# Stores, weights and a norm around the end of a recurrent head group: four moves in a hybrid diffusion step

## The chip, the cores and the metric

The kernel runs on one core of a Trainium2 chip. The metric is the time of one execution in microseconds (us), the median of several runs. Engine names: PE is TensorE (matrix products; PEld is its weight load), DVE is VectorE, ACT is ScalarE, POOL is GpSimd, SP is SyncE. Here SP, ACT and, after the change, POOL also issue DMA transfers, each in the order of its own queue.

## What is computed

One layer of a flow-matching backbone for 128 context tokens and 1024 latent tokens, all in float32. In the reference, cut to what matters here:

```python
h = rmsnorm(x, norm1_w) * (1 + sc1) + sh1
aq, ak, av, mq, mk, mv, mo, mg = split(h @ w_in)
attn_o = attention(q, keys, vals)                      # 8 heads of 64, softmax
hm = mlstm_bidir(q, k, v, gates, ...)                  # 4 heads of 128, two directions, chunks of 128
hm = rmsnorm(hm, mlstm_norm_w) * sigmoid(mo)
x = x + g1 * (concat([attn_o, hm]) @ w_out)
h2 = rmsnorm(x, norm2_w) * (1 + sc2) + sh2
x = x + g2 * (silu(gate) * up) @ w_down                # gate, up = h2 @ w_gu
y = rmsnorm(x, final_norm_w)
```

sh, sc and g come from a product of SiLU(cond) with `w_ada`; context and latent tokens have different ones. The final states of the context scan and the context's keys and values are outputs too.

## The kernel before

The 1152 tokens are nine blocks of 128: block 0 is the context, blocks 1 to 8 are latent. Three blocks make a chunk (chunks 0, 1, 2). Products are kept near float32 by splitting each operand into a high and a low part, so that one product is three matrix products (high x high, high x low, low x high). Splitting a weight takes a cast on ScalarE (`whi`, or `ir` for the early output weights) and a subtraction on VectorE (`wlo`, or `ir`); `load_piece` issues the load on SyncE's queue and then both.

The stages around the change, in order of the program:

1. `head_project(h)` makes q, k, v and the output gate of mLSTM head h for all blocks, and updates the chunk states block by block. It runs interleaved with the scan of head h - 1 and with attention of chunk 0. For every block it copies the transposed k (`kT`) out of PSUM on ScalarE.
2. `head_mlstm(h)` is the scan over the nine blocks. For a block it makes the decay weights (`dt` on ScalarE, `sd` on VectorE), the state part (`it` on ScalarE), the sum `nu`, the divisor `dn`, and the row `hm`, which GpSimd multiplies by the gate and, for finished blocks, by the norm factor (L897). The last head (`alone`) ends a chunk at a time and stores each chunk to the scratch tensor `hm_d[c]`: chunk 0 by SyncE's queue, chunks 1 and 2 by ScalarE's. The earlier heads store all chunks at the end by SyncE's queue.
3. Beside the last scan, `attn_out_first` multiplies chunk 0's attention output with the upper half of `w_out`, adds the gated result to x, and stores the residual rows to the scratch tensors `x1a_d[i]`. Its four weight pieces (two for each half n of the output columns) come by `load_piece`. The stores are collected in the list `stores` and issued on ScalarE's queue after the scan has been emitted. The `ada` generator streams more of `w_ada` at the same time.
4. `prefill` goes over blocks 0 to 8. `mix(b)` loads the block's row of `hm_d` (`hmr`, two ahead), transposes it on PE and splits it (`mx`). `half(b, n)` multiplies it with the lower half of `w_out` and adds the gated result. `end(b)` takes, for blocks 0 to 2, the mean square (`stats`), and emits the second norm (`norm2`) of chunk 0's block b - 1. `norm2` scales the row (`y`), transposes it on PE, applies scale and shift (`fl`) and splits it (`aTh`, `aTl`). Attention of chunk 1 is interleaved.
5. The feed-forward over the chunks follows, with `w_gu` and `w_down` streamed.

The program is written as generators that are interleaved by `weave`; the order on each engine is then set at build time by a scheduler that follows a simulated timeline and prefers older instructions, or those raised by `hot(n)`. Tiles of one tag are handed out in the order of the program; in these stages PSUM has three or four banks of the tag `mm`. Each engine works strictly in its order, so an instruction whose data are late holds all behind it, and a DMA issue that waits holds its queue's engine. `tc.issue_after(ins)` puts what is written inside it behind `ins` in the order of the engine of `ins`, without a wait for it.

Of the kernel before, what the change touches and what calls it, by code (L numbers as in the profile page):

```python
# [8 lines left out]
F32 = mybir.dt.float32  # L9
# [10 lines left out]
P = 128  # L20
# [8 lines left out]
NH = 4  # L29
# [4 lines left out]
CB = 3  # L34
NCH = NB // CB
CT = CB * P
# [9 lines left out]
def hybrid_step(ctx: ExitStack, tc: tile.TileContext, I: dict, O: dict):  # L46
    nc = tc.nc
    mm = nc.tensor.matmul
    act = nc.scalar.activation
    dve = nc.vector  # L50
    pool = nc.gpsimd
    dma = nc.sync.dma_start
# [46 lines left out]
    drp = ctx.enter_context(tc.tile_pool(name="drp", bufs=1, space=DRAM, reuse_waits="tile"))  # L99
# [4 lines left out]
        return psum["mm"].tile([P, 512], F32, name=nm("mm"), tag="mm")  # L104

    q_d = [drp.tile([P, 512], F32, name=f"q_d{b}") for b in range(NB)]
    hm_d = [drp.tile([CT, 512], F32, name=f"hm_d{c}") for c in range(NCH)]
    g_d = drp.tile([2, 2, D], F32, name="g_d")
    x1a_d = [drp.tile([P, D], F32, name=f"x1a_d{i}") for i in range(CB)]
    x1_d = [drp.tile([P, D], F32, name=f"x1_d{i}") for i in range(CB)]  # L110
# [633 lines left out]
    def head_project(h, st):  # L744

        w = groups_in[h + 1]
        pieces = w.made or w.pairs()
        w.inverses()
        nxt_steps = groups_in[h + 2].ready() if h + 1 < NH else iter(())
        next(nxt_steps, None)  # L750
        st["q"] = [None] * NCH
        st["b"] = [None] * NB

        def evac(b, ps):
            kt = mlp.tile([P, P], F32, name=nm("kt"), tag="kt", bufs=2)
            act(kt, ps[:, 0:P], AF.Copy, scale=w.inv_k)
            va = mlp.tile([P, P + 1], F32, name=nm("va"), tag="va", bufs=MB)
            act(va[:, 0:P], ps[:, P : 2 * P], AF.Copy, scale=w.inv)
            pool.memset(va[:, P : P + 1], 1.0)
            th = mlp.tile([P, P], F32, name=nm("th"), tag="th", bufs=1)  # L760
            act(th, ps[:, 2 * P : 3 * P], AF.Tanh, scale=w.inv_half)
            so = mlp.tile([P, P], F32, name=nm("so"), tag="so", bufs=MB)
            pool.tensor_tensor(out=so, in0=th, in1=mwh[:, h * P : (h + 1) * P], op=ALU.mult)
            pool.tensor_tensor(out=so, in0=so, in1=mwh[:, h * P : (h + 1) * P], op=ALU.add)
            pt = bank()
            transpose(pt[:, 0:P], kt)
            kT = mlp.tile([P, P], F32, name=nm("kT"), tag="kT", bufs=MB)
            nc.scalar.copy(kT, pt[:, 0:P])
            st["b"][b] = (kT, va, so)
            update(b, kt, va)  # L770

        st["s"] = states = {}
        st["raw"] = raws = {}
        for d in range(2):
            c0 = mlp.tile([P, P + 1], F32, name=nm("c0"), tag=("c0f", "c0b")[d], bufs=2 - d)
            dma(c0[:, 0:P], I["state_C"][0, 0, d, h])
            dma(c0[:, P : P + 1], I["state_n"][0, 0, d, h].rearrange("(p o) -> p o", o=1))
            states[d, 1 if d == 0 else NBL] = c0

        def update(b, kt, va):  # L780

            wv = mlp.tile([P, 2, P + 1], F32, name=nm("wv"), tag="wv", bufs=2)
            for d in range(2):
                pool.tensor_tensor(out=wv[:, d], in0=va, in1=qcol(1, d, b, h).to_broadcast([P, P + 1]), op=ALU.mult)
            pc = bank()
            mm(pc[:, 0 : 2 * (P + 1)], kt, wv.rearrange("p d x -> p (d x)"), start=True, stop=True)
            for d in range(2):
                if b == (NBL if d == 0 else 1):
                    continue
                add = pc[:, d * (P + 1) : (d + 1) * (P + 1)]  # L790
                cn = mlp.tile([P, P + 1], F32, name=nm("cs"), tag="cs", bufs=CSB)
                if d == 0 and b > 0:
                    dve.scalar_tensor_tensor(out=cn, in0=states[0, b], scalar=decb[:, b * 4 + h : b * 4 + h + 1], in1=add,
                                             op0=ALU.mult, op1=ALU.add)
                    states[0, b + 1] = cn
                    continue
                nc.scalar.copy(cn, add)
                if b > 0:
                    raws[b] = cn
                    continue  # L800
                dma(O["new_state_C"][0, 0, d, h], cn[:, 0:P])
                dma(O["new_state_n"][0, 0, d, h].rearrange("(p o) -> p o", o=1), cn[:, P : P + 1])

        def q_group(cs):
            banks = [bankA() for _ in cs]
            for k in range(KD):
                wh, wl = pieces[k // 2]
                for ps, c in zip(banks, cs):
                    mm(ps[:, 0:CT], wh[:, k % 2, 0:P], hTh[c][:, k, :], start=(k == 0), stop=False)
                    mm(ps[:, 0:CT], wh[:, k % 2, 0:P], hTl[c][:, k, :], start=False, stop=False)  # L810
                    mm(ps[:, 0:CT], wl[:, k % 2, 0:P], hTh[c][:, k, :], start=False, stop=(k == KD - 1))
                yield
            for ps, c in zip(banks, cs):
                qT = mlp.tile([P, CT], F32, name=nm("qT"), tag="qTm", bufs=2 * NCH)
                dve.tensor_scalar(out=qT, in0=ps[:, 0:CT], scalar1=w.inv, scalar2=None, op0=ALU.mult)
                st["q"][c] = qT

        for c in range(NCH):
            yield from q_group((c,))
        for i, _ in enumerate(linear_tok(pieces, P, 3 * P, evac, SINGLES)):  # L820
            if i % 6 == 5:
                next(nxt_steps, None)
            yield
        emit(nxt_steps)

    def head_mlstm(h, st):
# [30 lines left out]
        for b in range(NB):  # L857
# [34 lines left out]
            if b in ends:  # L892
                b0 = ends[b]
                n = b + 1 - b0
                v = hm[:, b0 : b + 1, :]
                r = rsqrt(mlp, ssh[:, b0 : b + 1], n, 1.0 / P)
                pool.tensor_tensor(out=v, in0=v, in1=bc(r, 2, [P, n, P]), op=ALU.mult)  # L897
                for c in range(b0 // CB, b // CB + 1):
                    (nc.scalar.dma_start if h == NH - 1 and c > 0 else dma)(hm_d[c][:, h * P : (h + 1) * P].rearrange("(b p) n -> p b n", p=P), hm[:, c * CB : (c + 1) * CB, :])
            yield  # L900


# [247 lines left out]
    def prefill(cur, nxt):  # L1150
# [4 lines left out]
        def load_hm(b):  # L1155
            if b >= NB:
                return None
            hm = xp.tile([P, 512], F32, name=nm("hmr"), tag="hmr", bufs=2)
            dma(hm, hm_d[b // CB][b % CB * P : (b % CB + 1) * P, :])
            return hm  # L1160

        def load_x1(b):
# [41 lines left out]
        def end(b):  # L1204
            if b < CB:
                with hot(200):
                    cur["rs"] += stats(x1s[0][b : b + 1])
            if 0 < b <= CB:
                yield from norm2(0, cur, b - 1)

        for b in range(2):
            mix(b)
# [15 lines left out]
                yield  # L1228
            yield from end(b)

    def attn_out_first(oT, ready, stores):


        x1 = hTp.tile([P, CB, D], F32, name="x1a", tag="hT2")
# [15 lines left out]
        def out():  # L1250
            for n in range(2):
                cs = slice(n * 512, (n + 1) * 512)
                ws = []
                for j in range(2):
                    rows = w_out[2 * j * P : (2 * j + 2) * P, cs].rearrange("(a p) n -> p a n", p=P)
                    ws.append(load_piece([(full_view, rows)], (2, 512), raw=raws[j], own=(his[j], los[j])))
                for cnd in range(2):
                    dma(gt[:, 2 * n + cnd], g_d[0, cnd : cnd + 1, cs].to_broadcast([P, 512]))
                yield
                for i in range(CB):  # L1260
                    while i not in ready:
                        yield
                    th, tl = mx[:, i, 0:4], mx[:, i, 4:8]
                    if n == 0:
                        dma(x1[:, i], xrow(i))
                        nc.scalar.copy(th, oT[i])
                        sub(tl, oT[i], th.bitcast(F32), "pool")
                        yield
                    ps = out_block([ws], 0, th, tl)
                    v = x1[:, i, cs]  # L1270
                    dve.tensor_tensor(out=gt[:, 4], in0=ps, in1=gt[:, 2 * n + (i > 0)], op=ALU.mult)
                    pool.tensor_tensor(out=v, in0=v, in1=gt[:, 4], op=ALU.add)
                    yield
                    if n == 1:
                        stores.append((x1a_d[i], x1[:, i]))

        return out(), ada

# [166 lines left out]
    oT = []  # L1445
# [5 lines left out]
        weave(head_project(h, sts[h]), beside((scan, 0.42), (att, 0.11)), 96, 96)  # L1451
        emit(scan)
    scan = head_mlstm(NH - 1, sts[NH - 1])
    stores = []
    first, ada = attn_out_first(oT, done, stores)
    emit(att)
    oT = []
    att = attention(1, oT, set())
# [1 line left out]
    emit(first)  # L1460
    emit(ada)
    emit(scan)
    for out, v in stores:
        nc.scalar.dma_start(out, v)
    es1.close()
    es_wp.close()
    es_d.close()
# [121 lines left out]
```

## Time and profile before

| | |
|---|---|
| median of 3 runs | 1564.69 us (1562.04 to 1565.68) |
| profiled execution | 1563.28 us, span of its instructions 1561.5 us |
| mean clock granted to TensorE | 0.98 |
| busy: PE, PEld, DVE, ACT, POOL | 1484.1, 1251.8, 1017.1, 772.3, 264.9 us |
| DMA queue of SyncE | 384670 packets, 230.26 MB |
| DMA queue of ScalarE | 3096 packets, 5.16 MB |

The profile is one execution. Busy time counts instructions of an engine; waits are put down to the event that came last. A row of the timeline has the start, the length, the engine, the line of the program, the operation, what it writes and reads, and, in brackets, how long the engine had been idle and what ended it. ACTq, SPq and POOLq are DMA issues or waits on those engines. The last head's scan ends near 506 us of the span; `prefill` lies between about 496 and 600 us, the feed-forward behind it.

### The profile page before, as it was taken

How to read it: one execution, taken by the hardware profiler on the slowest of the kernel's cores; microseconds unless marked ns; L12 is line 12 of the kernel's file. 1: busy time of each engine (PE TensorE's matmuls, PEld its weight loads, DVE VectorE, ACT ScalarE, POOL GpSimd, SP SyncE). 2: the span in 40 equal slices, each digit the busy share in tenths (PEclk: the TensorE clock that was granted, in tenths of full speed). 3: DMA queues.
4: the chain of work that ended last, by engine and by line, in shares of the span. 5: the costliest groups of instructions: out<-in, count | busy, mean ns of one | idle time of the engine just before them, and what ended most of it. 6: DMA issues, size and time to landing. Idle time of an engine off the chain costs nothing.

```text
span 1561.5 us, 23390 instructions
## 1 busy us (share of the span) xinstructions
PE 1484.1 (95%) x8539; PEld 1251.8 (80%) x8539; DVE 1017.1 (65%) x2009; ACT 772.3 (49%) x1413; POOL 264.9 (17%) x352
## 2 busy tenths in 40 slices
PE   6799999999988799999999999999999999999997
PEld 3545567677756679899998989989898989999996
DVE  4977555837648674878655577887866584554554
ACT  4854466847644553555432444556552443323333
POOL 0212423322434242000110101000010101001110
PEclk9999999999999799999999999999999999999999
DMA  9664423523356656797654447878763545544441
GB/s 365 201 179 158 85 70 41 120 49 55 79 183 207 201 111 186 192 192 186 151 151 151 142 132 248 185 169 188 176 159 114 169 131 173 162 121 136 148 141 62
DMA packets 387881, 236.91 MB, mean 152 GB/s; under 512 B 170198, under 2 KB 346790, under 8 KB 387766
## 3 DMA queue, kind: packets, MB, share of 16 engines
q1 hardware_dynamic: 384670, 230.26, 54.6%
q10 hardware_dynamic: 3096, 5.16, 1.3%
q8 instruction: 67, 1.10, 0.3%
q14 instruction: 48, 0.39, 0.1%
HBM read 183.79 MB, written 13.26 MB: 126 GB/s over the span
## 4 chain that ended last, share of the span: by engine, by line
PE 58%; DVE 3%; DMA 1%; ACT 1%; issue 0%; POOL 0%; ACTq 0%; DVEq 0%
PE mm L1341 11%; PE mm L1342 11%; PE mm L1340 11%; PE mm L1117 5%; PE mm L1118 5%; PE mm L1119 5%; PE S L1037 3%; PE po L1062 2%; PE po L1061 1%; PE mm L1145 1%; PE mm L1146 1%; PE mm L1147 1%; DVE wlo L137 1%; DMA raw<-in_w_gu_dram 1%; DVE fl L1329 1%; DVE t L1106 1%
## 5 line engine op out<-in xcount | busy, mean ns | idle before, releaser
L152 ACT CAST whi<-raw 128x1024 fp32r<-128x1024 f32 (+1 forms) x216 | 221.7, 1027 | 386.5 <-PE mm L1341 151.0
L137 DVE TENSOR_TENSOR wlo<-raw,whi 128x1024 fp32r<-128x1024 f32 (+1 forms) x216 | 260.1, 1204 | 178.9 <-ACT whi L152 176.3
L1341 PE MATMUL mm<-aTl,whi 128*128 128x384 f32 x1056 | 355.6, 337 | 2.7 <-DVE aTl L137 2.7
L1342 PE MATMUL mm<-aTh,wlo 128*128 128x384 f32 x1056 | 354.3, 336 | 0.0
L1340 PE MATMUL mm<-aTh,whi 128*128 128x384 f32 x1056 | 353.1, 335 | 0.0
L137 POOL TENSOR_TENSOR hl<-tn,hl 128x384 fp32r<-128x384 f32 x66 | 82.5, 1251 | 847.4 <-ACT hl L1363 776.3
L1341 PEld LDWEIGHTS mm<-aTl,whi 128*128 128x128 f32 x1056 | 198.5, 188 | 4.0 <-DVE aTl L137 3.4
L1340 PEld LDWEIGHTS mm<-aTh,whi 128*128 128x128 f32 x1056 | 198.2, 188 | 0.6
L1342 PEld LDWEIGHTS mm<-aTh,wlo 128*128 128x128 f32 x1056 | 198.4, 188 | 0.1
L1118 PE MATMUL mm<-wlo,hl 128*128 128x512 f32 x372 | 145.6, 391 | 0.0
L1117 PE MATMUL mm<-whi,hl 128*128 128x512 f32 x372 | 144.3, 392 | 0.0
L1119 PE MATMUL mm<-whi,hl 128*128 128x512 f32 x372 | 142.9, 392 | 0.0
L483 PE MATMUL wi<-ipair,hT 128*128 128x384 f16 (+2 forms) x408 | 135.0, 334 | 5.2 <-ACT vall L493 2.8
L484 PE MATMUL wi<-ipair,hT 128*128 128x384 f16 (+2 forms) x408 | 135.0, 334 | 0.0
L485 PE MATMUL wi<-ipair,hT 128*128 128x384 f16 (+2 forms) x408 | 131.6, 334 | 1.0 <-DVE hT L137 1.0
L1044 DVE SCALAR_TENSOR_TENSOR pl<-pr,st,ph 128x1152 f16<-128x1152 f32 (+1 forms) x72 | 96.6, 1342 | 34.5 <-ACT ph L1043 33.0
L1039 DVE TENSOR_REDUCE st<-S 128x1 f32<-128x1152 f32 (+1 forms) x72 | 88.9, 1234 | 15.7 <-PE S L1037 14.8
L1040 ACT ACTIVATE pr<-S,st 128x1152 f32<-128x1152 f32 (+1 forms) x72 | 81.4, 1131 | 31.7 <-DVE st L1039 31.0
L1043 ACT ACTIVATE ph<-pr,st 128x1152 f16<-128x1152 f32 (+1 forms) x72 | 83.8, 1163 | 25.5 <-DVE st L1042 12.7
L1037 PE MATMUL S<-kst,qT 128*128 128x384 f32 (+1 forms) x400 | 87.4, 352 | 1.3 <-ACT pr L1040 0.7
L1106 DVE TENSOR_TENSOR t<-mm,gl 128x512 f32<-128x512 f32 x102 | 68.7, 685 | 27.7 <-DMA gl<-g_d 12.2
L1119 PEld LDWEIGHTS mm<-whi,hl 128*128 128x128 f32 x372 | 69.9, 188 | 14.4
(381 smaller groups left out, 2525.3 us busy)
## 6 DMA issues: line engine op xcount, KB each, us to landing
raw<-in_w_gu_dram SPq DMA_DIRECT2D x132, 512.0 KB
raw<-in_w_down_dram SPq DMA_DIRECT2D x60, 512.0 KB
a<-in_w_ada_dram SPq DMA_DIRECT2D x24, 512.0 KB
gl<-g_d SPq DMA_DIRECT2D x36, 256.0 KB
aw<-in_w_ada_dram SPq DMA_DIRECT2D x16, 512.0 KB
iraw<-in_w_in_dram SPq DMA_DIRECT2D x32, 256.0 KB
raw<-in_w_out_dram SPq DMA_DIRECT2D x12, 512.0 KB
x<-in_x_sample_dram SPq DMA_DIRECT2D x11, 512.0 KB
```

Source lines behind the costliest of these rows:

```text
L137: (dve if eng == "dve" else pool).tensor_tensor(out=out, in0=full, in1=hi, op=ALU.subtract)
L152: nc.scalar.copy(hi[:, :n], raw[:, :n])
L483: mm(ps[:, :n], ah, wh[:, k % 2, c0 : c0 + n], start=(k == 0), stop=False)
L484: mm(ps[:, :n], ah, wl[:, k % 2, c0 : c0 + n], start=False, stop=False)
L485: mm(ps[:, :n], al, wh[:, k % 2, c0 : c0 + n], start=False, stop=(k == KD - 1))
L1037: mm(S[:, n, 0:w], qT[:, h, :], kst[kv][:, t, c0 + n * w : c0 + (n + 1) * w], start=(t == 0), stop=(t == 1))
L1117: mm(ps, ah, wh[:, k % 2, :], start=(k == 0), stop=False)
L1118: mm(ps, ah, wl[:, k % 2, :], start=False, stop=False)
L1119: mm(ps, al, wh[:, k % 2, :], start=False, stop=(k == nk - 1))
L1340: mm(ps, wh[:, k, :], th[:, k, :], start=(k == 0), stop=False)
L1341: mm(ps, wh[:, k, :], tl[:, k, :], start=False, stop=False)
L1342: mm(ps, wl[:, k, :], th[:, k, :], start=False, stop=(k == KD - 1))
```

## The change

It does four things.

- The chunks 1 and 2 of `hm_d` get another layout, one run of three blocks for each partition and head. The last head stores chunk 1 by ScalarE's queue as before and chunk 2 by GpSimd's. Rows of these chunks are loaded as four pieces of 128 numbers for each partition.
- The residual rows of chunk 0 are stored by GpSimd's queue right behind the addition that completes them; the list `stores` goes.
- The early output weights' casts are queued behind the last `kT` copy of the last head on ScalarE, and their subtractions behind its last forward state update on VectorE.
- `norm2` of block b is emitted at the end of block b + 2, not of block b + 1.

```diff
-    hm_d = [drp.tile([CT, 512], F32, name=f"hm_d{c}") for c in range(NCH)]
+    hm_d = [drp.tile([P, NH, CT] if c else [CT, 512], F32, name=f"hm_d{c}") for c in range(NCH)]
...
-            nc.scalar.copy(kT, pt[:, 0:P])
+            st["act"] = nc.scalar.copy(kT, pt[:, 0:P])
...
-                    dve.scalar_tensor_tensor(out=cn, in0=states[0, b], ...)
+                    st["dve"] = dve.scalar_tensor_tensor(out=cn, in0=states[0, b], ...)
...
                 for c in range(b0 // CB, b // CB + 1):
-                    (nc.scalar.dma_start if h == NH - 1 and c > 0 else dma)(hm_d[c][:, h * P : (h + 1) * P].rearrange("(b p) n -> p b n", p=P), hm[:, c * CB : (c + 1) * CB, :])
+                    if c == 0:
+                        dma(hm_d[0][:, h * P : (h + 1) * P].rearrange("(b p) n -> p b n", p=P), hm[:, 0:CB, :])
+                    else:
+                        ((None, nc.scalar.dma_start, pool.dma_start)[c] if alone else dma)(hm_d[c][:, h], hm[:, c * CB : (c + 1) * CB, :].rearrange("p b n -> p (b n)"))
...
-            dma(hm, hm_d[b // CB][b % CB * P : (b % CB + 1) * P, :])
+            if b < CB:
+                dma(hm, hm_d[0][b * P : (b + 1) * P, :])
+            else:
+                dma(hm.rearrange("p (h n) -> p h n", n=P), hm_d[b // CB][:, :, b % CB * P : (b % CB + 1) * P])
...
-            if 0 < b <= CB:
-                yield from norm2(0, cur, b - 1)
+            if 2 <= b < CB + 2:
+                yield from norm2(0, cur, b - 2)
...
-                    ws.append(load_piece([(full_view, rows)], (2, 512), raw=raws[j], own=(his[j], los[j])))
+                    with tc.issue_after(sts[-1]["act"].ins), tc.issue_after(sts[-1]["dve"].ins):
+                        ws.append(load_piece([(full_view, rows)], (2, 512), raw=raws[j], own=(his[j], los[j])))
...
                     if n == 1:
-                        stores.append((x1a_d[i], x1[:, i]))
+                        pool.dma_start(x1a_d[i], x1[:, i])
...
-    for out, v in stores:
-        nc.scalar.dma_start(out, v)
```

More of the change, by code (lines that the diff above doesn't have):

```diff
@@ L792, in update @@
                 if d == 0 and b > 0:
-                    dve.scalar_tensor_tensor(out=cn, in0=states[0, b], scalar=decb[:, b * 4 + h : b * 4 + h + 1], in1=add,
+                    st["dve"] = dve.scalar_tensor_tensor(out=cn, in0=states[0, b], scalar=decb[:, b * 4 + h : b * 4 + h + 1], in1=add,
                                              op0=ALU.mult, op1=ALU.add)
@@ L1229, in prefill, with attn_out_first @@
             yield from end(b)
-    def attn_out_first(oT, ready, stores):
+    def attn_out_first(oT, ready):
         x1 = hTp.tile([P, CB, D], F32, name="x1a", tag="hT2")
@@ L1453, in hybrid_step @@
     scan = head_mlstm(NH - 1, sts[NH - 1])
-    stores = []
-    first, ada = attn_out_first(oT, done, stores)
+    first, ada = attn_out_first(oT, done)
     emit(att)
```

## Prediction

> **What bounds the kernel now.** I read the page's slices first, then the waits of PE over the whole execution, then the windows. In the slices each digit is a tenth of 39 us.
>
> ```profile
> PE   6799999999988799999999999999999999999997
> PEclk9999999999999799999999999999999999999999
> ```
>
> PE is nearly always busy, except in the slices around 430 to 550 us; the one 7 of the clock row lies there too (508 to 547 us). The waits of PE (total, times, longest) and two windows (length, then busy us of PE, PEld, DVE, ACT, POOL, clock, DMA share, GB/s) say the same:
>
> ```profile
> PE mm L116 <- ACT y L1319: 8.8, 2, 7.9
> PE mm L1145 <- ACT mx L1185: 7.1, 1, 7.1
> PE mm L116 <- ACT it L870: 6.0, 3, 3.5
> ...
> 500.00:600.00 100.00, 80.23 (x395) 66.77 (x393) 67.41 (x146) 48.10 (x74) 36.33 (x26) 0.86 0.64 167
> 600.00:700.00 100.00, 99.39 (x565) 93.36 (x564) 70.67 (x93) 53.52 (x69) 11.63 (x9) 1.00 0.79 195
> ```
>
> The three longest totals are waits of PE for ScalarE, and the 100 us behind them have PE 99% busy. So PE is the bound behind this stage, and each microsecond by which the last head and the `prefill` pass end earlier should arrive at the end. I take the three waits in order of time.
>
> **The output weights behind the last copy.** The two pieces of `w_out` for the early output blocks are cast on ScalarE (`ir`). The timeline (start, us, engine, line, operation, idle before it and releaser):
>
> ```profile
> 450.11 1.04 ACT L152 CAST ir<-ip 128x1024 fp32r<-128x1024 f32 x1 [3.38 <-DMA ip<-in_w_out_dram]
> ...
> 451.67 0.63 ACT L870 ACTIVATE it<-mm,QT 128x129 f32<-128x129 f32 x2
> 452.35 0.33 PE L116 MATMUL mm<-ident,kt 128*128 128x128 f32 x1 [3.46 <-ACT it L870]
> ...
> 458.07 0.27 ACT L768 COPY kT<-mm 128x128 f32<-128x128 f32 x1
> ...
> 467.47 0.48 PE L1145 MATMUL mm<-ir,mxa 128*128 128x512 f32 x1
> ```
>
> The first cast stands in ScalarE's order ahead of `it` and waits 3.38 us for its load; PE waits behind both from 448.9 to 452.35. With the cast queued behind the last `kT` copy, PE waits for the two operations of `it` alone, which take 0.63 us: about 0.7 us instead of 3.46. That is 2.8 us. What PE does next ran at a lowered clock:
>
> ```profile
> 450.00:460.00 10.00, 6.80 (x36) 4.65 (x36) 6.27 (x17) 6.70 (x19) 1.84 (x5) 0.83 0.77 271
> ```
>
> (1 - 0.83) x 10 = 1.7 us lost to the clock, which goes if the wait becomes 0.7 us. Gross 4.5 us. Against it: two casts (1.04 us each) and two subtractions on VectorE (1.23 us each, row below) leave idle time and come between the last copy and the last head's scan, whose exponentials and `sd` products PE waits for. The first `w_out` product stands 9.4 us behind the copy, so the weights themselves are in time. Bounds: nothing, if they run behind the scan's first work, to 4.6 us, if all four stand ahead of it. I take one cast, 1.0 us, since the scan's instructions are older in the program. **Net 3.5 us** (0 to 4.5).
>
> **The last head's stores.** Behind the scan:
>
> ```profile
> 502.35 1.98 ACT L152 CAST whi<-raw 128x1024 fp32r<-128x1024 f32 x2
> 505.94 1.23 DVE L137 TENSOR_TENSOR wlo<-raw,whi 128x1024 fp32r<-128x1024 f32 x1
> 506.14 1.71 POOL L897 TENSOR_TENSOR hm<-hm,ry 128x384 f32<-128x384 f32 x1 [3.16 <-DVE ry L133]
> 507.88 0.38 ACTq L899 DMA_DIRECT2D hm_d<-hm  x1
> 508.30 1.07 ACT L1185 CAST mx<-mm 128x512 fp32r<-128x512 f32 x2 [3.97 <-POOL hm L897]
> 508.92 1.29 DVE L137 TENSOR_TENSOR mx<-mm,mx 128x512 fp32r<-128x512 f32 x2 [1.75 <-ACT mx L1185]
> 508.94 0.80 PE L1145 MATMUL mm<-whi,mx 128*128 128x512 f32 x1 [7.14 <-ACT mx L1185]
> ...
> 510.81 0.63 PE L1147 MATMUL mm<-whi,mx 128*128 128x512 f32 x1
> ```
>
> The casts `mx` of blocks 0 and 1 need nothing of chunk 2. They wait 3.97 us because the store of chunk 2 stands ahead of them on ScalarE's queue and waits for GpSimd's L897. On GpSimd's queue that store waits only behind the operation that makes its data, and its readers (blocks 6 to 8) come after block 3, whose rows PE takes at 546.91 (row below). ScalarE then goes on at 504.33 and the first L1145 at about 505.0. The third product, L1147, needs VectorE's `mx` half, and VectorE is busy with `wlo` until 507.17; half of 1.29 us later it is 507.8, against 510.81. So **3.0 us** (1.7 by VectorE's order, 508.92 against 507.17, to 3.9 by ScalarE's). PE still idles some 3 us, and I count no gain of clock.
>
> SyncE's queue has the same knot (its own waits, and the timeline):
>
> ```profile
> SPq L151 <- DMA hm_d<-hm: 8.0, 1, 8.0
> ...
> 512.19 0.90 SPq L151 DMA_DIRECT2D raw<-in_w_out_dram  x2
> ```
>
> The loads of the second half of the weights go out only when that store has landed, 4.3 us after its issue, though they share no tile. With the store off the two hardware queues I expect this wait to become the one for `wlo`, at 507.2. If it stays, the second halves of blocks 0 and 1 take the 3.0 us back.
>
> **The norm two blocks late.**
>
> ```profile
> 513.18 0.90 SPq L1159 DMA_DIRECT2D hmr<-hm_d  x2
> ...
> 525.07 0.40 PE L1147 MATMUL mm<-whi,mx 128*128 128x512 f32 x1
> ...
> 525.78 0.68 DVE L1106 TENSOR_TENSOR t<-mm,gx_all 128x512 f32<-128x512 f32 x1
> ...
> 533.41 1.97 PE L116 MATMUL mm<-ident,y 128*128 128x128 f32 x8 [7.95 <-ACT y L1319]
> ...
> 535.17 1.06 PE L116 MATMUL mm<-ident,hmr 128*128 128x128 f32 x4
> ...
> 530.00:540.00 10.00, 5.94 (x21) 5.17 (x22) 5.92 (x31) 7.92 (x14) 1.30 (x2) 0.50 0.27 78
> ```
>
> Block 0's sum goes through VectorE, GpSimd, a square with its sum, and a chain of small VectorE operations before `y` is there. PE has block 2's rows (loaded from 513.18) but takes them only after the norm, since the PSUM banks of the tag go round in program order. With the norm behind block 2's products, PE can transpose block 2 once the bank of block 0's second half is free (526.46), then wait for one cast and one subtraction (0.5 to 0.6 us each, halves of the `mx` rows). 1.0 + 0.6 and 1.5 for the subtraction with what stands before it make 3.1 us of idle time instead of 7.95. That is 4.9 us, with 24 products to fill the rest. Clock: in 530 to 540 PE was busy 5.94 us at 0.50, so 3.0 us lost; whether a gap of 3.1 us lowers it, an earlier stretch must say:
>
> ```profile
> PE mm L844 <- DVE sd L852: 2.3, 1, 2.3
> ...
> 460.00:470.00 10.00, 7.66 (x49) 5.49 (x48) 7.46 (x29) 3.55 (x14) 4.10 (x4) 0.83 0.37 113
> ```
>
> Here the longest wait was 2.3 us and the clock still fell to 0.83, so I take 2.0 of the 3.0. Against the gain stands VectorE, which has to serve the same work in less time (67 of 100 us busy on average here): 1.5 us. **Net 5.4 us** (0 to 8).
>
> The Trainium skill (TensorE: Matmul & The Clock Gate, Part 1) has the clock halve only after an idle window of about 3.4 us. By that rule alone all 3.0 us would come back and the sum below would be one microsecond better; the 2.3 us wait above does not bear it out, and I stay with the rows.
>
> The norm's last block is now two products later, but the feed-forward starts behind block 8, four blocks on, so it costs nothing unless that cover goes.
>
> **Residual rows by GpSimd's queue, and runs.** No DMA issue on GpSimd is in this trace. The nearest rows are ScalarE's issue of such a store and GpSimd's neighbours:
>
> ```profile
> 488.32 1.27 POOL L1272 TENSOR_TENSOR x1a<-x1a,gta 128x512 f32<-128x512 f32 x1
> 493.41 1.28 POOL L1272 TENSOR_TENSOR x1a<-x1a,gta 128x512 f32<-128x512 f32 x1 [1.51 <-DVE rt L131]
> 494.73 0.33 ACTq L1464 DMA_DIRECT2D x1a_d<-x1a  x1
> 495.64 0.83 POOL L897 TENSOR_TENSOR hm<-hm,ry 128x384 f32<-128x384 f32 x1 [0.94 <-DVE ry L133]
> ```
>
> Let a store hold GpSimd for h: 0.33 us if like ScalarE's, 4.3 us if until it lands. The second store comes between 494.69 and L897 at 495.64, and behind L897 wait the store of chunk 1 on ScalarE's queue and the scan's last exponentials. I take 1.3 us, one GpSimd operation, so 0.4 us over the gap. **Cost 0.5 us**; at 4.3 us the delay is 2h - 4.7 = 3.9 us (the first store then also pushes the second add). ScalarE loses three stalling issues, whose gain lies in the waits above. The runs: a store of chunk 1 or 2 becomes one run for each partition, cheaper if anything, and its load becomes four runs of 512 bytes.
>
> ```profile
> 536.26 0.34 SPq L1159 DMA_DIRECT2D hmr<-hm_d  x1
> ...
> 546.91 0.60 PE L116 MATMUL mm<-ident,hmr 128*128 128x128 f32 x4
> ...
> raw<-in_w_gu_dram SPq DMA_DIRECT2D x132, 512.0 KB
> ...
> 612.87 4.28 DMA raw<-in_w_gu_dram
> ```
>
> A gate weight piece is 512 KB in such runs and lands in 4.28 us (the chain that ended last); an `hmr` half that size has 10.6 us. Nothing.
>
> **Sum.** -3.5 - 3.0 - 5.4 + 0.5 = -11.4 us. The profiled execution took 1563.28 us (span 1561.5 and 1.8 around it), which gives 1551.9; the median of the runs is 1.4 above it, so 1553.3.
>
> **Rivals.**
>
> More than that: the gaps left at the second and third place stay too short for the clock to drop. The slice at 0.7 lost 0.3 x 39 = 11.7 us to the clock, with PE 7 tenths busy: 8.2 us. Of the 6.2 not yet counted I give this case 4.6, and VectorE's 1.5 us: -17.5, 1547.2. For it: both causes of the low clock, the waits of 7.1 and 7.9 us, shrink by more than half. Against it: VectorE's `wlo` order holds PE near 508, and the 2.3 us wait above.
>
> The norm's move fills nothing: the norm runs at raised priority, and should the program's order decide less than I read, PE still stops for `y`; or VectorE sets the pace. Then -6.0, 1558.7. Against it: PE took block 2 behind the norm though its rows were there.
>
> Gains given back: the four weight operations all stand ahead of the scan and the norm fills nothing: -2.4, 1562.3, within 0.2% (3.1 us, about what a measurement of this kernel can tell from no change).
>
> Slower: GpSimd's queue. With h above 3.8 us each store pushes the next, L897, ScalarE's store of chunk 1 and the last exponentials: 2h - 4.7. It eats the 11.9 us from h = 8.3 on; at h = 10 it costs 15.3, so +3.4 us, 1568. For it: GpSimd slows beside VectorE, L897 taking 1.71 us instead of 0.83. Against it: that is a factor of two on 1.3, and even the landing is 4.3.
>
> The Trainium skill (SBUF — State Buffer, the box "DVE blocks DMA") has GpSimd build such descriptors itself and wait while VectorE holds a shared port: 620 ns became about 3100 ns. At h = 3.1 the second store would end at 497.8, L897 would be 2.1 us late, and the time 1554.9, an estimate from that page. No run here shows it yet; it speaks against the change, but not enough to turn its sign.
>
> **How the numbers follow.** Forecast 0.52, with its own range 1549 to 1557; more gain 0.15; no gain from the norm 0.17; given back 0.06; slower 0.10. The range 1545 to 1561 holds the first three and leaves out 0.16. Faster by over 0.2%: 0.52 + 0.15 + 0.17 = 0.84; within: 0.06; slower: 0.10.
>
> **What would show it.** In the changed profile: no wait of PE for `it` above 1 us near 449; `mx` on ScalarE right behind the two `whi` casts; the second pair of `raw` loads near the end of `wlo`, not behind a landing of `hm_d`; PE's transposes of block 2 ahead of the first `y` and no wait of 8 us for `y`; GpSimd's issues of 1 to 2 us. The prediction is wrong if PE's idle time between 440 and 600 falls by less than 5 us, if a new wait of PE for `ir`, `sd` or `hmr` of that size appears there, or if the windows behind 600 lose their 99%.

## The result, and the profile after

| | before | after |
|---|---|---|
| median of the runs, us | 1564.78 (1562.04 to 1566.23) | 1554.76 (1553.14 to 1557.40) |
| ratio, 95% interval | 1 | 0.9945 (0.9933 to 0.9958) |
| profiled execution, us (span) | 1563.28 (1561.5) | 1556.62 (1554.8) |

The kernel became faster by 8.6 us by the ratio (0.0055 of 1565), with bounds of 6.6 and 10.5; the medians lie 10.0 us apart. The two profiled executions lie only 6.7 us apart: before's is below its median and after's above. Executions of one kernel differ by some 4 us, in one kernel below by 8.9, so the ratios carry the verdicts, and the profiles show where time goes. How far single profiles can be trusted is seen ahead of the `it` near 442 us: ScalarE and VectorE run the same operations in the same order up to there in all fourteen kernels, and reach it between 441.6 and 445.0 us. In the listing after, lines have moved: L1145 to L1147 are now L1148 to L1150, L1185 is L1191, L1107 is L1110, L1061 is L1064, L1037 is L1040, L1319 is L1326.

The slices of the page, the waits of PE over the whole execution (total, times, longest) and the windows, as they were shown of before:

```profile
PE   6799999999988899999999999999999999999997
PEclk9899999999999899999999999999999999999998
...
PE mm L1148 <- ACT mx L1191: 7.7, 3, 5.9
PE po L1064 <- DMA phT<-ph: 5.9, 1, 5.9
...
500.00:600.00 100.00, 84.78 (x427) 70.79 (x428) 70.64 (x151) 50.04 (x77) 40.47 (x31) 0.91 0.67 184
600.00:700.00 100.00, 97.74 (x566) 90.65 (x565) 70.91 (x99) 54.61 (x72) 8.15 (x7) 1.00 0.73 181
```

The slice that showed 7 for busy and for clock shows 8 in both. In 500 to 600 us PE is busy 84.78 us instead of 80.23, at 0.91 instead of 0.86. The wait of 7.9 us for `y` is gone from the list. A wait of 5.9 us for `phT`, the transposed weights of the attention, is new.

The timeline at the three places of the prediction (start, us, engine, line, operation, idle before it and releaser):

```profile
449.49 0.33 PE L116 MATMUL mm<-ident,kt 128*128 128x128 f32 x1 [0.32 <-ACT it L870]
...
503.92 1.04 ACT L152 CAST whi<-raw 128x1024 fp32r<-128x1024 f32 x1
504.87 1.07 ACT L1191 CAST mx<-mm 128x512 fp32r<-128x512 f32 x2
505.50 0.80 PE L1148 MATMUL mm<-whi,mx 128*128 128x512 f32 x1 [5.91 <-ACT mx L1191]
506.42 1.17 SPq L151 DMA_DIRECT2D raw<-in_w_out_dram  x2
...
508.62 0.80 PE L1150 MATMUL mm<-whi,mx 128*128 128x512 f32 x1 [1.04 <-DVE mx L137]
...
517.14 0.60 PE L116 MATMUL mm<-ident,hmr 128*128 128x128 f32 x4
...
529.22 2.20 POOL L1110 TENSOR_TENSOR x<-x,t 128x512 f32<-128x512 f32 x1 [2.22 <-DVE t L1109]
...
530.26 1.17 DVE L131 TENSOR_TENSOR rt<-ry 128x1 f32<-128x1 f32 x1
531.35 0.15 DVE L1044 RECIPROCAL st<-st 128x1 f32<-128x1 f32 x1
532.37 1.26 ACT L1046 ACTIVATE ph<-pr,st 128x1152 f16<-128x1152 f32 x1 [2.56 <-DVE st L1045]
533.66 1.30 SPq L1049 DMA_TRANSPOSE phT<-ph  x1
535.64 1.33 ACT L1326 ACTIVATE y<-x,ry 128x512 f32<-128x512 f32 x2 [0.97 <-DVE ry L133]
537.08 0.40 PE L1064 MATMUL po<-phT,vs 128*128 128x256 f16 x1 [5.89 <-DMA phT<-ph]
537.27 1.92 PE L116 MATMUL mm<-ident,y 128*128 128x128 f32 x8
538.98 1.06 PE L116 MATMUL mm<-ident,hmr 128*128 128x128 f32 x4
```

First place: PE waits 0.32 us for `it`, not 3.46. Second: the two `mx` casts stand right behind the `whi` casts, and no longer wait for L897 of chunk 2, and the second pair of `raw` loads goes out at 506.42 instead of 512.19. Third: PE takes block 2's rows at 517.14, 20 us ahead of block 0's `y`. So each of these edits does what it says; the residual rows' stores are looked at below. The reader should also see what stands ahead of block 3's rows (538.98): the first product of the attention's values, which waits for `phT`, and then `y`, which was itself only made at 535.64.

### The profile page after: what moved, and what is told of

Same layout as the page of the kernel before. It is cut to its first block, busy times and chain, and to the rows that moved or that the text cites. A ratio compares the mean times of both kernels' runs of the same rounds, so it can differ in the third digit from the quotient of the medians.

```text
span 1554.8 us, 23400 instructions
## 1 busy us (share of the span) xinstructions
PE 1482.2 (95%) x8539; PEld 1247.6 (80%) x8539; DVE 1015.6 (65%) x2009; ACT 773.1 (50%) x1413; POOL 266.6 (17%) x356
## 4 chain that ended last, share of the span: by engine, by line
PE 59%; DVE 4%; DMA 1%; ACT 1%; issue 0%; ACTq 0%
PE mm L1348 11%; PE mm L1349 11%; PE mm L1347 11%; PE mm L1120 5%; PE mm L1121 5%; PE mm L1122 5%; PE S L1040 3%; PE po L1064 1%; PE po L1065 1%; PE mm L1148 1%; PE mm L1150 1%; PE mm L1149 1%; DMA raw<-in_w_gu_dram 1%; DVE wlo L137 1%; DVE fl L1336 1%; DVE x L1110 1%
## 5 line engine op out<-in xcount | busy, mean ns | idle before, releaser
L1120 PE MATMUL mm<-whi,hl 128*128 128x512 f32 x372 | 144.2, 392 | 0.0
L1122 PE MATMUL mm<-whi,hl 128*128 128x512 f32 x372 | 142.8, 392 | 0.0
L1042 DVE TENSOR_REDUCE st<-S 128x1 f32<-128x1152 f32 (+1 forms) x72 | 88.8, 1233 | 15.8 <-PE S L1040 15.2
L1040 PE MATMUL S<-kst,qT 128*128 128x384 f32 (+1 forms) x400 | 86.6, 349 | 1.4 <-ACT pr L1043 1.1
L1122 PEld LDWEIGHTS mm<-whi,hl 128*128 128x128 f32 x372 | 69.9, 188 | 14.4
```

Source lines behind the costliest of these rows:

```text
L1040: mm(S[:, n, 0:w], qT[:, h, :], kst[kv][:, t, c0 + n * w : c0 + (n + 1) * w], start=(t == 0), stop=(t == 1))
L1120: mm(ps, ah, wh[:, k % 2, :], start=(k == 0), stop=False)
L1122: mm(ps, al, wh[:, k % 2, :], start=False, stop=(k == nk - 1))
```

## The experiments

All ratios are against runs of the kernel before taken beside them; 0.001 is 1.56 us. Their intervals reach 0.0009 to 0.0019 to each side, mostly 0.0012, or 2 us. A difference between two of these ratios is known to some 2.5 us.

**One part undone at a time**, the other three kept as in the changed kernel.

The weights (the two ordering edges taken out again):

```
-                    with tc.issue_after(sts[-1]["act"].ins), tc.issue_after(sts[-1]["dve"].ins):
-                        ws.append(load_piece(...))
+                    ws.append(load_piece(...))
```

> The changed kernel with the output weights' casts free to stand anywhere again (as before the change), everything else kept. Changed kernel: 1554.8 us. Theory 1, the terms add up as forecast: the loss of the 3.5 us term gives 1558.3 us, and PE's wait for `it` near 449 is back at 3.5 us. Rival, the term was won near 450 and given back before 500 (chunk 0 of the last head is stored at 488.7 in the changed kernel against 481.8 before): 1554 to 1556 us, although the wait for `it` is back.

Measured: 0.9980 (0.9972 to 0.9989), 1560.61 us. Undoing it loses 5.5 us (3.1 to 7.8), more than the forecast term, and the wait for `it` is back at 3.5 us as theory 1 had it. The rival's 1554 to 1556 us are ruled out.

The store of chunk 2:

```
-                        ((None, nc.scalar.dma_start, pool.dma_start)[c] if alone else dma)(hm_d[c][:, h], ...)
+                        ((None, nc.scalar.dma_start, nc.scalar.dma_start)[c] if alone else dma)(hm_d[c][:, h], ...)
```

> The changed kernel with the store of chunk 2 on ScalarE's queue again (layout of runs kept). Theory 1: 3.0 us lost, 1557.8 us; `mx` waits for L897 again by 3 to 4 us, and the second pair of output weight loads for a landing of `hm_d`. Rival: PE's wait of 5.9 us for the attention's `phT` near 531, which is not fed by `mx`, ends last, so the earlier `mx` only lengthens that wait: 1554 to 1555.5 us.

Measured: 0.9943 (0.9931 to 0.9954), 1554.02 us: no loss is seen, and one of 3.0 us lies just outside what the two intervals allow. `mx` on ScalarE does wait for L897 again, by 4.40 us. The waits of PE between 440 and 600 us show what came of it:

```profile
PE mm L1148 <- ACT mx L1191: 10.4, 2, 10.2
PE po L1064 <- DMA phT<-ph: 4.5, 2, 2.8
PE mm L116 <- ACT y L1326: 3.3, 1, 3.3
```

PE stands 10.2 us for `mx` instead of 5.9 and the time is the same; the longest wait for `phT` is 2.8 us instead of 5.9, and one of 3.3 for `y` stands beside it. That disagrees with the forecast of 3.0 us and agrees with the rival: here an earlier `mx` lengthens the wait for `phT` instead.

The norm:

```
-            if 2 <= b < CB + 2:
-                yield from norm2(0, cur, b - 2)
+            if 0 < b <= CB:
+                yield from norm2(0, cur, b - 1)
```

> The changed kernel with the norm one block behind again. Theory 1: 5.4 us lost, 1560.2 us, and a wait of PE for `y` of about 8 us. Rival: the gap was only exchanged for the 5.9 us wait for `phT`, so that 2 us are lost, 1556.8 us, and in this run the wait for `phT` is gone while the one for `y` is back.

Measured: 0.9986 (0.9974 to 0.9997), 1561.53 us, a loss of 6.4 us (3.8 to 9.1). The time is theory 1's (5.4), not the rival's (2). As the rival said, the wait for `phT` is gone and that for `y` is back, with one for the attention's exponentials beside it (waits of PE between 440 and 600 us, and the window):

```profile
PE mm L116 <- ACT y L1326: 8.0, 1, 8.0
...
PE S L1040 <- ACT pr L1043: 4.3, 2, 3.6
...
500.00:600.00 100.00, 80.73 (x396) 67.06 (x396) 69.65 (x151) 48.43 (x77) 34.52 (x30) 0.88 0.62 168
```

But the exchange was not as even as the rival had it: the window has 4.0 us less of busy PE than that of the changed kernel, at 0.88 instead of 0.91.

The residual rows:

```
-                        pool.dma_start(x1a_d[i], x1[:, i])
+                        stores.append((x1a_d[i], x1[:, i]))
...
     emit(scan)
+    for out, v in stores:
+        nc.scalar.dma_start(out, v)
```

> The changed kernel with the three residual row stores on ScalarE's queue behind the scan again (chunk 2's store stays on GpSimd's queue). Theory 1, a cost of 0.5 us for them on GpSimd: 1554.3 us. Rival, the 2.8 and 2.6 us for which GpSimd stands ahead of the second and third store delay the scan's L891 and L897, and that ate the gain of the weights: 1551 to 1553 us, with chunk 1's L897 2 to 4 us earlier than 502.7.

Measured: 0.9955 (0.9938 to 0.9971), 1555.21 us, no difference from the changed kernel within the intervals, so neither the 0.5 us of theory 1 nor its opposite is shown; the rival's gain did not come. Chunk 1's L897 does come 2.8 us earlier, counted from the `it` at 442.76 in the changed kernel and at 441.82 here (502.67 - 442.76 = 59.9 against 498.90 - 441.82 = 57.1), and the time doesn't follow.

**One part done alone**, on the kernel before. The edits are the same, the other way round. The weights alone:

> The kernel before with the output weights' casts behind the last copy, and nothing else. Theory, the two carrying parts add up: undoing this part alone cost 5.5 us, so doing it alone saves 3.5 (forecast) to 5.5 us: ratio 0.9965 to 0.9978. Rival, the parts need each other (what is won before 500 us is lost in the wait for `y` when the norm is one block behind): within 0.2% of before.

Measured: 0.9994 (0.9985 to 1.0002), 1563.83 us: 0.9 us, with bounds of -0.3 and 2.3. The rival's time is right, but not its place: the wait for `y` is 7.9 us as before. Waits of PE between 440 and 600 us, of before (where `mx` has 7.1 and `it` 3.5, as shown ahead) and then of this kernel:

```profile
PE mm L116 <- DMA hmr<-hm_d: 0.7, 1, 0.7
PE S L1037 <- ACT pr L1040: 0.7, 1, 0.7
```

```profile
PE mm L1145 <- ACT mx L1185: 7.9, 1, 7.9
PE S L1037 <- ACT pr L1040: 3.9, 2, 3.2
...
PE mm L116 <- DMA hmr<-hm_d: 1.5, 1, 1.5
...
PE mm L116 <- ACT it L870: 0.3, 1, 0.3
```

Some 3.2 us went from `it`, and 2.5 from `plT`, the other half of the attention's transposed weights (2.5 in the list of before, none in this one); 4.8 us are found again in three later waits: 0.8 at `mx`, 3.2 at `pr`, 0.8 at `hmr`. And the scan ends its first chunk later. Chunk 0's L897, of before and then of this kernel:

```profile
480.80 0.83 POOL L897 TENSOR_TENSOR hm<-hm,ry 128x384 f32<-128x384 f32 x1 [2.56 <-DVE ry L133]
```

```profile
486.46 0.83 POOL L897 TENSOR_TENSOR hm<-hm,ry 128x384 f32<-128x384 f32 x1 [0.23 <-DVE dn L884]
```

Counted from the `it` ahead of the last block's (442.48 and 444.70), that is 38.3 and 41.8 us: 3.4 us later, though the last block's `it` comes 3.1 earlier. Chunk 0's `hmr` is loaded from what is stored behind it.

The norm alone:

> The kernel before with the norm two blocks behind, and nothing else. Theory: 5.4 (forecast) to 6.4 us faster, ratio 0.996 to 0.9965. Rival: the store of chunk 2 on ScalarE's queue and the second weight loads behind its landing hold the products anyway, so that no more than 2 us come: ratio 0.9987 or more.

Measured: 0.9949 (0.9935 to 0.9963), 1557.01 us: 8.0 us, the whole gain but for what the intervals hide, and above the 5.4 to 6.4 of the theory. The rival is ruled out.

The weights and the norm:

> The kernel before with the weights' casts behind the last copy and the norm two blocks behind; stores, runs and residual rows as before. Theory, these two are the whole gain: ratio 0.9943 to 0.995, as the changed kernel (0.9945). Rival, the stores only looked idle when undone one at a time, and together they carry 2 to 3 us: ratio 0.996 or more.

Measured: 0.9951 (0.9938 to 0.9963), 1556.73 us. With the norm moved, the weights' edges add nothing (-0.3 us, within the intervals). The waits of PE between 440 and 600 us, first with the norm alone, then with both:

```profile
PE mm L1145 <- ACT mx L1185: 7.3, 1, 7.3
PE mm L116 <- ACT it L870: 4.5, 1, 4.5
PE po L1062 <- DMA plT<-pl: 3.0, 1, 3.0
...
PE po L1061 <- DMA phT<-ph: 1.6, 1, 1.6
```

```profile
PE mm L1145 <- ACT mx L1185: 9.8, 3, 8.1
PE po L1061 <- DMA phT<-ph: 6.2, 2, 5.8
```

With both, the wait for `it` is 0.3 us, so 4.2 go there; 2.5 come back at `mx` and 1.6 at the attention's two transposes (6.2 against 4.6).

The norm and the residual rows:

> The kernel before with the norm two blocks behind and the residual rows' stores on GpSimd's queue; chunk 2's store, the runs and the weights as before. The norm alone gave 0.9949, and with both changes of stores 0.998, so the two together cost 4.8 us where the weights are not moved. Theory, the held residual stores on GpSimd (up to 3.6 us ahead of the third, in front of the scan's last L891) make that cost: 0.997 to 0.9985. Rival, it comes with chunk 2's store on GpSimd's queue or the runs: 0.994 to 0.996.

Measured: 0.9945 (0.9926 to 0.9964), 1557.10 us. The rival is right: the held stores alone are not seen to cost anything. The two intervals would hide some 3 us, not 4.8. The six executions spread from 1554.36 to 1563.22. So the odd kernel is the one with the norm, both changes of stores and unmoved weights (0.9980). Whether chunk 2's store, the runs or their meeting with the residual rows makes it slower was not tried and stays open.

**GpSimd's stores.** Of the three residual stores GpSimd issues, the second and third begin 2.8 and 2.6 us after it had nothing else to do. The edit gives their descriptors more room:

```
-    nc = _bacc.Bacc("TRN2", ..., dynamic_dma_scratch_size=256)
+    nc = _bacc.Bacc("TRN2", ..., dynamic_dma_scratch_size=384)
```

> The changed kernel with half as much again of room for the descriptors of GpSimd's stores (384 bytes of a partition instead of 256). Theory R: the room of the changed kernel holds one store's descriptors, so GpSimd stands until the store before is read; with room for two the 2.76 and 2.58 us ahead of the second and third residual store fall under 0.5 us, and chunk 1's L897 comes 2 to 3 us earlier than 59.9 us behind the `it` of the block before. Rival D: GpSimd waits for its port or builds descriptors in that time, whatever the room: 2.5 to 2.8 us as before. The time: the changed kernel's (0.9945) under both, or up to 1.5 us better under R.

Measured: 0.9955 (0.9942 to 0.9969), 1558.02 us. The timeline of GpSimd in the changed kernel, and with more room:

```profile
488.65 0.71 POOL L1282 DMA_DIRECT2D x1a_d<-x1a  x1
...
490.82 1.28 POOL L1279 TENSOR_TENSOR x1a<-x1a,gta 128x512 f32<-128x512 f32 x1 [0.95 <-DVE gta L1278]
494.86 0.60 POOL L1282 DMA_DIRECT2D x1a_d<-x1a  x1 [2.76 <-issue]
...
499.34 0.58 POOL L1282 DMA_DIRECT2D x1a_d<-x1a  x1 [2.58 <-issue]
```

```profile
492.57 0.59 POOL L1282 DMA_DIRECT2D x1a_d<-x1a  x1 [0.31 <-POOL x1a L1279]
...
495.63 0.58 POOL L1282 DMA_DIRECT2D x1a_d<-x1a  x1 [0.42 <-POOL x1a L1279]
```

The hold falls to 0.31 and 0.42 us, so theory R holds. The landings say what is waited for. In the changed kernel the first store lands 5.89 us behind its issue, at 494.54, and the second 4.17 us behind, at 499.03; the held stores begin 0.31 us behind these. So do all fifteen held stores in the eight kernels that have any. With more room the second and third store begin 1.75 and 1.96 us ahead of the landing of the one before. Chunk 1's L897 comes 2.8 us earlier (501.87 - 444.72 = 57.1 from the same `it`), but again no time comes of it: the ratio is 0.001 above the changed kernel's, within the intervals.

**What is left.** In the changed kernel PE waits 5.9 us ahead of block 3's rows. One kernel takes the norm a block later still, one weaves the attention in more thinly, one does both:

```
-            if 2 <= b < CB + 2:
-                yield from norm2(0, cur, b - 2)
+            if 3 <= b < CB + 3:
+                yield from norm2(0, cur, b - 3)
```

```
-        due += 0.35
+        due += 0.25
```

The norm three blocks behind:

> The changed kernel with the norm three blocks behind instead of two. In its profile PE stands 5.9 us behind block 2's products for `phT`, because the first values of the attention and block 0's `y` stand ahead of block 3's rows. Theory, the order of the program decides what fills that gap: block 3's rows and 24 products (about 6 us at full clock) come ahead, the wait for `phT` falls to under 2 us, and 3 to 6 us are saved: ratio 0.9907 to 0.9925. Rival, the chain of the attention and the norm on VectorE and GpSimd sets the pace: the gap comes back one block later, and the time stays within 1.5 us of the changed kernel, 0.9935 to 0.9955.

The attention woven in more thinly:

> The changed kernel with the attention woven in more thinly (0.25 of its steps for each step of the pass instead of 0.35). PE then reaches block 0's `y` ahead of the first values. Theory, both of them are late at this place and either holds PE: a wait of 4 to 6 us for `y` takes the place of that for `phT`, and the time stays within 1.5 us, 0.9935 to 0.9955. Rival, the attention alone is too early: 3 us or more are saved, 0.9925 or less.

Both:

> The changed kernel with both: the norm three blocks behind and the attention woven in more thinly. Theory of the order: as with the norm three blocks behind alone, or up to 1.5 us better, since no value stands ahead of block 3's products: ratio 0.990 to 0.9925. Rival, the chains set the pace: 0.9935 to 0.9955.

Measured: 0.9945 (0.9933 to 0.9956), 0.9943 (0.9931 to 0.9955) and 0.9943 (0.9931 to 0.9955); medians 1555.14, 1553.85 and 1554.85 us. The three are as fast as the changed kernel and no faster. With the norm three blocks behind, PE takes block 3's rows at 530.03 and the wait for `phT` falls to 1.1 us. With the thinner attention the wait for `phT` falls to 0.5 us, and one of 5.5 for `y` takes its place:

```profile
530.03 0.60 PE L116 MATMUL mm<-ident,hmr 128*128 128x128 f32 x4
...
PE po L1064 <- DMA phT<-ph: 1.1, 1, 1.1
```

```profile
PE mm L116 <- ACT y L1326: 5.5, 1, 5.5
...
PE po L1064 <- DMA phT<-ph: 0.5, 1, 0.5
```

So in the times the rival is right for the first and the last, and the theory for the second. The order of the program decides which wait PE has, and no gain in time is seen from it; one of up to some 2.5 us would be hidden by the intervals. The one profiled execution of the norm three blocks behind took 175.9 us from the `it` to the attention's S products behind 620 us, against 180.6 in the changed kernel (how this is counted is told below); its median does not bear that out.

## Why the prediction was right

The time came 1.5 us above the forecast (1554.76 against 1553.3), inside its own range. The sign and the main mechanism were right: the norm's move fills PE's gap. The rival by which the gains are given back describes the weights and the store, but not the norm. But that the sum came out so near is in part luck: three of its four terms were mis-sized, and the errors cancelled. In the table a minus is time that the part saves, with what the intervals allow in brackets.

| term | forecast, us | done alone | undone from the changed kernel |
|---|---|---|---|
| output weights | -3.5 | -0.9 (0.3 to -2.3) | -5.5 (-3.1 to -7.8) |
| last head's stores | -3.0 | not tried | 0.3 (3.0 to -2.4), chunk 2's queue |
| norm two blocks late | -5.4 | -8.0 (-5.8 to -10.2) | -6.4 (-3.8 to -9.1) |
| residual rows by GpSimd | +0.5 | -0.6 on top of the norm, within the intervals | -1.6, within the intervals |

**Output weights.** The step that failed is the one from the wait to the path. Read at the wait, it was right: 0.32 us for `it` instead of 3.46. But the prediction's opening let each microsecond by which the stage ends earlier arrive at the end, and counted one won at its entrance as such. It was given back inside the stage, at `mx`, `pr` and `hmr`; what PE meets next is released, by the rows above, by ScalarE's casts and exponentials and by loads, not by PE. In the stretch from the `it` to 620 us that is cut into windows below, PE idles 27.6 us with the weights alone and 27.5 before; what fell there, in these single executions, is the time lost to the clock, from 10.8 to 8.7. The sum had kept 1.0 us for casts in the scan's way, where chunk 0's L897 came 3.4 us later, and its lower bound of nothing was nearer. A slip stands in the term as well: the 1.7 us of clock are 0.17 of the whole 10 us, where PE was busy for 6.80 of them, which gives 1.2. The 5.5 us on undoing it belong to the slower combination above, whose cause is open; there too the idle time is the same (23.3 us without the edges, 23.5 with them) and the loss to the clock 2.2 us larger.

**Last head's stores.** The reading of the knot was right: ScalarE went on at once, the first product came at 505.50 (forecast about 505.0), the third at 508.62 (507.8). Its worth was mis-sized: 3.0 us forecast, none measured for chunk 2's queue. PE's wait fell only from 7.14 to 5.91 us, since PE too came there earlier, and what follows block 2's products then waited for `phT`. SyncE's second loads went out 5.8 us earlier, but not at the end of `wlo` as forecast: ahead of them SyncE waited for the landing of a residual store, which the prediction had not put there (SyncE's own waits):

```profile
SPq L1170 <- DMA x1a_d<-x1a: 6.3, 1, 6.3
```

The runs were forecast at nothing and never shown apart from the store.

**Norm.** Only in this term the gain was larger than forecast. Between the `it` and the first of the attention's S products behind 620 us lies the same work in both kernels:

```profile
442.48 0.63 ACT L870 ACTIVATE it<-mm,QT 128x129 f32<-128x129 f32 x2 [1.38 <-PE mm L867]
...
630.14 1.33 PE L1037 MATMUL S<-kst,qT 128*128 128x384 f32 x6 [0.61 <-DVE qT L137]
```

```profile
443.18 0.63 ACT L870 ACTIVATE it<-mm,QT 128x129 f32<-128x129 f32 x2 [1.38 <-PE mm L867]
...
622.98 1.21 PE L1037 MATMUL S<-kst,qT 128*128 128x384 f32 x6
```

Each has 160 S products ahead of it. The first pair is before, 187.7 us apart; the second the norm alone, 179.8 apart, so 7.9 us less, and 8.0 less by the ratio. Cut into forty equal windows, each with its idle time of PE and its busy time multiplied by what the clock lacked to 1, before has 27.5 us idle, 10.8 lost to the clock and 149.3 of work; the norm alone has 22.7, 8.0 and 149.1. So 4.8 us are idle time (forecast 4.9) and 2.8 clock (forecast 2.0). Undoing the norm in the changed kernel says much the same: 186.4 us with 26.9 idle and 10.3 lost to the clock, against 180.6 with 23.5 and 7.1, so 3.5 us of idle time and 3.2 of clock. These are one execution each, and how close the first pair comes to the ratio is partly chance: the norm with the residual rows, profiled in an execution of 1563.2 us against a median of 1557.1, took 185.0 for the stretch. The 1.5 us charged for VectorE's pace are not seen in these sums. The Trainium skill's clock rule (TensorE: Matmul & The Clock Gate, Part 1), by which all 3.0 us of clock would return, was nearer than the 2.0 taken, in both pairs; these are sums over many gaps and do not test its threshold.

In the changed kernel the wait of 7.95 us became one of 5.9 for `phT`, not of 3.1 for a cast: that the attention's values could stand between block 2's products and block 3's rows was not in the prediction.

**GpSimd's stores.** A store held GpSimd for up to 3.4 us (0.60 of issue and 2.76 of standing), against the 1.3 taken and the 4.3 of the far bound. That bound had the right event, the landing, at the wrong place: GpSimd does not stand behind its own store but works on, and stands ahead of the next store until the one before has landed. Chunk 1's L897 came 2.8 us later for it, where 2h - 4.7 gives 2.0 at h = 3.36. The slower rival needed h above 8.3 and was far off. The figure of the Trainium skill (SBUF — State Buffer, the section "A bandwidth-pool intuition that's wrong (but worth ruling out)", behind the box "DVE blocks DMA"), about 3100 ns for a DMA of GpSimd's queue beside a copy on VectorE, is near the 3.36 us; its cause is not the one here. The holds ended with a landing, and VectorE was free for 0.9 us at the start of the first one, while more room for descriptors took it away:

```profile
493.00 0.69 DVE L1278 TENSOR_TENSOR gta<-mm,gta 128x512 f32<-128x512 f32 x1 [2.27 <-PE mm L1150]
```

GpSimd's add ended at 492.10, and VectorE began only at 493.00, after 2.27 us without work.

**What was to show it.** The windows from 440 to 500 us, of before and of after, go with those from 500 to 600 that stand ahead:

```profile
440.00:500.00 60.00, 52.87 (x336) 38.37 (x334) 40.24 (x120) 27.11 (x86) 21.13 (x28) 0.94 0.59 191
```

```profile
440.00:500.00 60.00, 54.02 (x343) 39.20 (x341) 39.03 (x118) 28.10 (x88) 22.77 (x30) 0.94 0.60 194
```

PE's idle time fell from 7.1 + 19.8 = 26.9 to 6.0 + 15.2 = 21.2 us, by 5.7, just past the limit of 5 below which the prediction was to be wrong. No new wait for `ir`, `sd` or `hmr` appeared; the new wait that did, for `phT`, was not on the list. One sign came out against the prediction: PE's busy time from 600 to 700 us, which was to keep its 99%, fell from 99.39 to 97.74, with a wait of 1.9 us for a product of the feed-forward (`tn`, on VectorE) that before does not have there. With the norm alone the window has 100.00, with the weights alone 97.49; what makes it was not tried.

## What to carry to other kernels

A wait that is taken away at the entrance of a stage is worth what the next waits leave of it: follow PE to the end of the stage and ask at each later wait whether its releaser gets earlier too. Here the step that gave PE other work to do while it would have waited (the norm behind a further block's products) brought 8.0 us of 8.6 by itself; the weights' edges, which only took a wait away, brought 0.9 by themselves, and undoing chunk 2's queue lost nothing. And undo each part as well as do each alone: the two answers differed by 4.6 us for the weights, so in this stage, where several chains end close together, the terms of the sum are not independent.

## What the runs showed of the hardware

A store of 128 runs on GpSimd's queue issued in 0.58 to 0.71 us, but one that was due before the store ahead of it had landed stood until 0.31 us behind that landing, up to 2.8 us in the changed kernel; the profile names nothing that it waited for. With 384 instead of 256 bytes of descriptor room it stood 0.31 and 0.42 us and began ahead of the landing. This fits room for one such store in the first case and two in the second. In the changed kernel with the weights' edges undone, the second store came 1.03 us behind the landing of the first and was not held, and the third stood 3.61 us.

The kernel with more room gained in the stage and lost it behind. From the first S product behind 620 us (621.60) to the end of its span (1557.9) it took 936.3 us, where the changed kernel took 931.5 (1554.8 - 623.33). The other kernels with the attention woven in as before took 931.3 to 932.8 for it. Between 700 and 1540 us the products of 128x512 of one kind (L1120 to L1122, some 343 of each) became slower, from 391 or 392 ns each to 395 or 396, which is about 4 us. This is one execution; the edit gives no reason for it, and the cause was not settled.

In the timeline of the result, a VectorE operation on 128 x 1 values took 1.17 us (L131 at 530.26; others of its kind take 0.15 to 0.23 in the next 10 us) beside a GpSimd addition that took 2.20 instead of 1.29 (L1110 at 529.22); both ended near 531.4. At 526.09 it took 0.92, and ended within 0.02 us of the addition that GpSimd began at 525.70. The attention's reciprocal queued behind it, and so `ph` and `phT`. That the two engines hold each other up there was read from the trace, not tested.
